# The second half's k, v and r kept in DRAM, and its recurrence set beside the first half's up projection

## The chip, the cores and the metric

The kernel runs on one core of a Trainium2 chip. The metric is the device time of one execution, in microseconds (us). TensorE (PE) multiplies, VectorE (DVE), ScalarE (ACT) and GpSimd (POOL) do the elementwise work, and SyncE (SP) issues every DMA. Each engine takes its own instructions strictly in the order in which they were laid down.

## What is computed

One layer of a block with a token mixer and a channel mixer over 1024 tokens of width 1024, all in float32:

```python
mod = silu(c) @ ada_w + ada_b                      # 6 vectors of 1024: modulation
sh_m, sc_m, gt_m, sh_f, sc_f, gt_f = split(mod, 6)
h = rms_norm(x, mix_pre_g) * (1 + sc_m) + sh_m
p = h @ w_in                                       # conv part, r, k, v, low-rank inputs
u = silu(layer_norm(causal_dwconv(u * sigmoid(u_gate), 31 taps)))
y = wkv7_scan(r, decay, k, v, kk, a)               # per head, state 64 x 64, token by token
y = (layer_norm(y) + bonus) * g
x = x + gt_m * rms_norm(concat([u, y]) @ w_out)
h = rms_norm(x, ffn_pre_g) * (1 + sc_f) + sh_f
z_gate, z_val = split(causal_dwconv(h @ w_up, 3 taps), 2)
x = x + gt_f * rms_norm((silu(z_gate) * z_val) @ w_down)
```

## The kernel before

The tokens are cut into two halves of 512 columns (`half` 0 and 1), and for the recurrence into four quarters of 256 (`q` 0 to 3), of four chunks of 64 tokens each. Everything lies with features on the 128 partitions and tokens along the free axis.

**Projections.** `project` (L147) multiplies one 128-row output tile. Float32 accuracy comes from two rounded parts of each operand (`hh`, `hl` for the activations, `wh`, `wl` for the weights) and three matmuls per 128 inputs, so a tile with 1024 inputs is 24 matmuls of 512 columns. `weight` (L135) loads 512 columns of weights (a chunk, two to a tile), ACT rounds them (L140), POOL takes the difference (L142); three buffers in a ring hold each of the three forms. The first half's `w_in` tiles are `lora`, `in_group` (k, v, r), `gate_in`, `glu`; then the same for the second half; then `out_proj`, `channel_in`, `up` (44 tiles `up_tile`) and `down`, for each half.

**Recurrence.** For each quarter `unit` does `prep` for two groups of heads (`w`, `a` and decay products, the kk norm, the chunk matrices `s`), `inverse` (a triangular inverse by DVE with a trip through DRAM, tensors `sa` and `sd`) and `merge` (`pt`, `hn`). Then `chain` walks the four chunks one after the other: `ch` (PE), `rs` (DVE L680 and ACT), `ch` again, `uv`, `y`, `zv`, each of which waits for the one ahead, and the state `zv` goes from quarter to quarter. `finish` normalizes y (`rx_y` at L173 is its first step) and writes it to DRAM (`mixed`, printed `mx`), where `mix_in` fetches it for `out_proj`.

**Convolution.** `conv` is a filler: DVE adds 93 taps of 3 channel tiles in a PSUM bank and ACT and POOL those of a fourth, some taps each time that `shifted`, `glu` or `up_tile` asks for a piece; `conv_norm` ends it.

**Modulation.** The first two of the six vectors come at the start (`ada_cols` on `ada1`). The other four are groups 0 to 3 of `ada2`: eight column blocks of eight 256 KB loads, each followed by one DVE step (`cacc_b` at L235 and L237), four small matmuls (`adrb`, L243) and an addition. They are the iterator `spare`, of which `project` takes `rate` steps after each weight chunk, and their loads share the weights' ring of three buffers (`wp`, tag `w`, printed `w_adb`).

**Order.** The program is written top to bottom (L888 to L966), but a scheduler lays down each engine's order, by a simulated time line and by priorities: earlier code goes first among what is ready, `first()` lifts a block by 1,000,000 places, `tc.high_priority(offset=500000)` by half as many. Before the change all of the recurrence, units and chains of all four quarters, is under `first()`. Buffers of a tag are taken in the order of the code. k and r tiles have three buffers each, v six, so the second half's k, v and r wait until the first half's quarters are done with theirs.

Of the kernel before, what the change touches and what calls it, by code (L numbers as in the profile page):

```python
# [10 lines left out]
ALU = mybir.AluOpType  # L11
# [56 lines left out]
def build(nc, tc, I, O):  # L68
# [151 lines left out]
    def ada_cols(j, src, name, pool, tag, bufs, apool, atag, b="m", share=()):  # L220
# [22 lines left out]
            TE.matmul(ps[:, m:m + 1], acc[:, m * P:(m + 1) * P], ones, start=True, stop=True)  # L243
        V.tensor_tensor(mod[:, j:j + 4], ps[:, 0:4], col("ada_b", j, 4), ALU.add)

    h = [None] * NK
    started = {}
    def start(z):
# [46 lines left out]
    def shifted(ps, half, j, out, n=P):  # L295

        q = tmp(f"s{half}_{j}", HT + 1)
        if half == 0:
            G.memset(q[:n, 0:1], 0.0)
        else:  # L300
            G.tensor_copy(q[:n, 0:1], carry_q[:n, j:j + 1])
        S.activation(q[:n, 1:], ps[:n], AF.Identity, scale=col("mu", j)[:n], bias=ZERO[:n])
        outs = out if isinstance(out, list) else [out]
        w = HT // len(outs)
        for i, o in enumerate(outs):
            V.scalar_tensor_tensor(o, ps[:n, i * w:(i + 1) * w], om[:n, j:j + 1], q[:n, i * w:(i + 1) * w], ALU.mult, ALU.add)
        if half == 0:
            G.tensor_copy(carry_q[:n, j:j + 1], q[:n, HT:HT + 1])
        next(filler[0], None)
# [80 lines left out]
            nc.sync.dma_start(mixed[half][ct], accs[ct])  # L390

    def lora(h, half):
        la = rw.tile([P, HT], F32, name=f"la{half}", tag="la", bufs=1)
# [59 lines left out]

    def v_tiles(half):

        new = lambda q, g: rw.tile([P, 2, QT], F32, name=f"v{2 * half + q}{g}", tag="v", bufs=6)
        order = ((0, 0), (0, 1), (1, 0), (1, 1)) if half == 0 else ((0, 0), (1, 0), (0, 1), (1, 1))
        t = {(q, g): new(q, g) for q, g in order}
        return [[t[q, g] for q in range(2)] for g in range(2)]

    def in_group(h, half, g, v):

        def new(x, q):
            if half == 0 and g == q == 1:
                return shared_slot({"k": "cacc1", "r": "cacc3"}[x], f"{x}{half}{g}")
            return rw.tile([P, 2, QT], F32, name=f"{x}{2 * half + q}{g}", tag=x, bufs=3)
        kvr = [[new("k", q) for q in range(2)], v, [new("r", q) for q in range(2)]]
        for i in range(2):
            p = 2 * g + i
            for x in range(3):  # L470
                shifted(in_tile(h, 10 + 3 * p + x, f"{'kvr'[x]}{half}{p}"), half, (4, 8, 0)[x] + p, [t[:, i] for t in kvr[x]])
        return kvr

    class Group:
# [287 lines left out]
    def x_rstd(half):  # L762

        acc = None
        for k in range(NK):
            x = tmp(f"xs{half}_{k}")
            nc.sync.dma_start(x, I["xT"][half, k])
            acc = square_sum(acc, x, k, f"x{half}")
        return rstd(acc, f"x{half}", ones, 1, 1.0 / D, EPS_RMS)

    def out_proj(half, ins):

# [105 lines left out]
    def unit(q, kvrs, la, before=None):  # L878

        pcs = wk.tile([P, 4, 4], F32, name=f"pc{q}", tag="pc", bufs=2)  # L880
        gs = [prep(q, g, kvrs[g], la, pcs, sas[q % 2]) for g in range(2)]
        inverse(q, sas[q % 2], sd[q % 2])
        if before:
            finish(q - 1, *before)
# [14 lines left out]
    with first():  # L899
        u0 = unit(0, kvrs, la)  # L900
        ys, zv = chain(0, *u0, None)
    ada = lambda gs: (x for g in gs for z in range(2)
                      for x in ada_cols(16 + 8 * g + 4 * z, I["ada2"][g, z], f"b{g}{z}", wp, "w", 3, cv, "cacc2"))
    spare, rate = ada(range(3)), 3
    for ct in range(4):
        glu(h, 0, ct)
        if ct == 0:
# [6 lines left out]
    for x in xs:  # L914
        V.tensor_tensor(x, x, rb, ALU.mult)
    h = [modulate(x, gm[:, k:k + 1], mod[:, k:k + 1], f"1_{k}") for k, x in enumerate(xs)]
    accs = [None] * 4
# [9 lines left out]
    with tc.high_priority(offset=500000):  # L927
        gates = gate_in(h, 1)
    for ct in range(4):
        glu(h, 1, ct)  # L930
        if ct == 0:
# [10 lines left out]
    for _ in spare:  # L942
        pass
# [6 lines left out]
    spare = ada((3,))  # L950
    filler[0] = conv(1, accs, 3)
    up(h, 0, lambda j: j == 18 and conv_norm(accs, 1, "s"))
    V.tensor_tensor(gpf, mod[:, 40:48], col("ffn_post_g", 0, 8), ALU.mult)
    oin = mix_in(1)
    cv.release()
# [68 lines left out]
```

## Time and profile before

| | us |
|---|---|
| median of 3 runs (1515.91 to 1520.45) | 1516.82 |
| the profiled execution | 1514.99 |
| its span, first to last instruction | 1513.2 |
| PE busy | 1377.6 |
| DVE busy | 958.3 |
| POOL busy | 796.4 |
| ACT busy | 645.9 |

An execution of 1514.99 us holds the span of 1513.2 and 1.8 us around it. A busy PE counts matmuls that overlap in its pipeline, so it says when PE had work, not that it was at its peak; the granted clock (PEclk) stands beside it, as a share of 2.4 GHz, and half of it is 1.2 GHz.

### The profile page before, as it was taken

The page shows a single profiled execution, that of the slowest core. Times are in us where ns is not written, and L with a number is a line of the kernel's source. Part 1 is how long each engine was busy: PE and PEld are TensorE (multiplying, and loading weights), DVE is VectorE, ACT ScalarE, POOL GpSimd, SP SyncE. Part 2 cuts the span into 40 slices and gives each one's busy share as a digit, 9 for nine tenths or more (in the row PEclk, how much of TensorE's full clock was granted, in tenths as well). Part 3 has the DMA queues.
Part 4 walks back from the last instruction along what each step waited for, and adds up shares of the span by engine and source line. Part 5 has one row for each costly group of instructions (what it writes and reads, how often), then busy time and mean ns, then how long its engine had stood idle before and what let it go on. Part 6 is the DMA issues. An engine that isn't in the chain of part 4 may idle for free.

```text
span 1513.2 us, 22723 instructions
## 1 busy us (share of the span) xinstructions
PE 1377.6 (91%) x8148; PEld 1111.8 (73%) x8148; DVE 958.3 (63%) x1449; ACT 645.9 (43%) x1126; POOL 796.4 (53%) x710
## 2 busy tenths in 40 slices
PE   3999868789889999769999999999998999999995
PEld 2777657677667777657788887788886888888884
DVE  8657857969989576587889965557117555552102
ACT  5344322355534454344455555654233444443221
POOL 2555413676755346435577764446545555554443
PEclk9998998899999999869999999999999999999997
DMA  9153645533224544834444335884335333333332
GB/s 358 58 167 101 176 140 160 175 81 105 63 60 118 162 138 107 219 116 128 138 132 133 118 120 179 303 274 134 101 97 185 98 97 97 97 95 93 94 95 73
DMA packets 161761, 203.78 MB, mean 135 GB/s; under 512 B 63536, under 2 KB 70320, under 8 KB 161648
## 3 DMA queue, kind: packets, MB, share of 16 engines
q1 hardware_dynamic: 161648, 202.33, 43.4%
q8 instruction: 64, 1.05, 0.3%
q14 instruction: 49, 0.40, 0.1%
HBM read 168.19 MB, written 34.08 MB: 134 GB/s over the span
## 4 chain that ended last, share of the span: by engine, by line
PE 66%; DVE 17%; DMA 10%; issue 3%; SPq 2%; POOL 2%; ACT 1%; DVEq 0%; POOLq 0%; ACTq 0%
PE up L158 10%; PE up L159 9%; PE up L160 9%; PE d L159 5%; PE d L160 5%; PE d L158 5%; DMA w_adb<-ada 3%; DVE cv L344 2%; PE o L159 2%; PE o L158 2%; PE o L160 2%; DMA aw_ada<-ada 2%; DVE cacc_b L237 1%; DVE rkp L528 1%; SPq L625 1%
## 5 line engine op out<-in xcount | busy, mean ns | idle before, releaser
L142 POOL TENSOR_TENSOR wl_up<-w_up,wh_up 128x512 fp32r<-128x512 f32 x176 | 240.3, 1370 | 157.5 <-ACT wh_up L140 150.7
L158 PE MATMUL up<-hh_f,wh_up 128*128 128x512 f32 x704 | 278.6, 396 | 10.2 <-DVE q_za L815 7.0
L159 PE MATMUL up<-hl_f,wh_up 128*128 128x512 f32 x704 | 277.0, 394 | 0.0
L160 PE MATMUL up<-hh_f,wl_up 128*128 128x512 f32 x704 | 276.6, 393 | 0.0
L140 ACT CAST wh_up<-w_up 128x512 fp32r<-128x512 f32 x176 | 108.7, 619 | 187.0 <-PE up L159 127.6
L142 POOL TENSOR_TENSOR wl_dn<-w_dn,wh_dn 128x512 fp32r<-128x512 f32 x96 | 116.9, 1220 | 118.0 <-ACT wh_dn L140 112.0
L158 PEld LDWEIGHTS up<-hh_f,wh_up 128*128 128x128 f32 x704 | 133.9, 190 | 40.6 <-issue 9.8
L160 PEld LDWEIGHTS up<-hh_f,wl_up 128*128 128x128 f32 x704 | 133.6, 190 | 28.2 <-issue 0.2
L159 PEld LDWEIGHTS up<-hl_f,wh_up 128*128 128x128 f32 x704 | 133.7, 190 | 27.6
L159 PE MATMUL d<-al,wh_dn 128*128 128x512 f32 x352 | 139.4, 396 | 0.0
L160 PE MATMUL d<-ah,wl_dn 128*128 128x512 f32 x352 | 139.4, 396 | 0.0
L158 PE MATMUL d<-ah,wh_dn 128*128 128x512 f32 x352 | 139.2, 395 | 0.0
L344 DVE SCALAR_TENSOR_TENSOR cv<-cu,pv,cv 128x512 f32<-128x512 f32 x174 | 130.4, 749 | 2.4
L140 ACT CAST wh_dn<-w_dn 128x512 fp32r<-128x512 f32 x96 | 56.1, 584 | 151.3 <-PE d L159 123.7
L860 DVE TENSOR_SCALAR mo_f<-d,mod 128x512 f32<-128x512 f32 x16 | 12.0, 749 | 170.4 <-ACT q_sqd L859 159.1
L810 DVE SCALAR_TENSOR_TENSOR q_za<-up,pv,q_za 128x510 f32<-128x510 f32 x88 | 65.6, 746 | 78.4 <-ACT q_za L808 78.4
L352 POOL TENSOR_TENSOR cacc<-cacc,ctmp 128x512 f32<-128x512 f32 x60 | 79.1, 1318 | 42.3 <-ACT ctmp L351 38.7
L159 PEld LDWEIGHTS d<-al,wh_dn 128*128 128x128 f32 x352 | 66.2, 188 | 16.0
L160 PEld LDWEIGHTS d<-ah,wl_dn 128*128 128x128 f32 x352 | 66.2, 188 | 15.8
L158 PEld LDWEIGHTS d<-ah,wh_dn 128*128 128x128 f32 x352 | 66.2, 188 | 15.8
L838 DVE SCALAR_TENSOR_TENSOR q_za<-q_th,q_za 128x512 f32<-128x512 f32 x44 | 57.7, 1312 | 30.3 <-ACT q_th L837 30.3
L815 DVE SCALAR_TENSOR_TENSOR q_za<-up,pv,q_za 128x511 f32<-128x511 f32 x88 | 65.9, 748 | 14.0 <-ACT carry_z L814 8.3
(383 smaller groups left out, 3024.5 us busy)
## 6 DMA issues: line engine op xcount, KB each, us to landing
w_up<-w_up SPq DMA_DIRECT2D x176, 256.0 KB, 2.8
w_dn<-w_down SPq DMA_DIRECT2D x80, 256.0 KB, 2.7
w_adb<-ada SPq DMA_DIRECT2D x64, 256.0 KB, 3.0
aw_ada<-ada SPq DMA_DIRECT2D x32, 256.0 KB, 5.4
w_o<-w_out SPq DMA_DIRECT2D x32, 256.0 KB, 3.5
act<-q_za SPq DMA_DIRECT2D x22, 256.0 KB, 2.0
ax<-act SPq DMA_DIRECT2D x22, 256.0 KB, 4.2
w_ug<-w_in SPq DMA_DIRECT2D x16, 256.0 KB, 3.1
```

The source lines that it names most:

```text
L140: S.copy(hi, w)
L142: e.tensor_tensor(lo, w, hi.bitcast(F32), ALU.subtract)
L158: TE.matmul(ps, wh[:, o], xh, start=k == 0, stop=False)
L159: TE.matmul(ps, wh[:, o], xl, start=False, stop=False)
L160: TE.matmul(ps, wl[:, o], xh, start=False, stop=k == K - 1)
L237: V.scalar_tensor_tensor(acc, w, sc[:, k:k + 1], acc, ALU.mult, ALU.add)
L344: yield V.scalar_tensor_tensor(o, u[:, k:k + HT], cw(ct, k), acc, ALU.mult, ALU.add)
L352: G.tensor_tensor(acc, acc, t, ALU.add)
L528: V.tensor_tensor(pic(rkp[x][:, :, 1 + hh, :])[r], part(kkn, x)[r], half(eprev, x)[r], ALU.mult)
L810: V.scalar_tensor_tensor(a[:, 2:], ps[:, 0:HT - 2], fw(0), a[:, 2:], ALU.mult, ALU.add)
L815: V.scalar_tensor_tensor(a[:, 1:], ps[:, 0:HT - 1], fw(1), a[:, 1:], ALU.mult, ALU.add)
L838: V.scalar_tensor_tensor(g_, t, 1.0, g_, ALU.add, ALU.mult)
```

## The change

It has five parts.

1. `ada_rest` takes the place of `ada_cols` for the four later vectors. Its loads go to five buffers of the convolution's pool that lie idle at the time (tags `ctmp` twice, `cu`, `cu3`, `cacc0`), four loads ahead of their use; the running sum lies in PSUM bank `v`. It is `spare` from the second group of the first half on (rate 1, then 2 in `glu`), not from `glu` on (rate 3). The small matmuls' result goes to PSUM bank `s`, of which there is one, where `prep` puts `w`, the kk norm and the bonus.
2. k, v and r of the second half are written to DRAM as whole tiles (`group_out`, 12 writes) and fetched by quarter (`group_back`, 12 loads); a second `la` buffer; v has five buffers.
3. `first()` is taken from units 2 and 3, chains 2 and 3 and the last `finish`; the `finish` inside a unit gets it. The half-as-high priority is taken from the second half's projections.
4. `out_proj(0)` and `channel_in(0)` stand ahead of chain 2, unit 3, chain 3 and the last `finish`, which in turn stand ahead of `up(h, 0)`.
5. The last vector's steps begin at the ninth pair of tiles of `up`, in the buffers of k. The row sums of `x_rstd` go to bank `y`.

```diff
+    def ada_rest(groups, slab, ahead, last, b):
+        todo = [(g, z, k) for g in groups for z in range(2) for k in range(NK)]
+        tiles = {}
...
+        for i in range(ahead):
+            fetch(i)
+        for i, (g, z, k) in enumerate(todo):
+            fetch(i + ahead)
+            w, name = tiles.pop(i), f"b{g}{z}"
+            if k == 0:
+                acc = bank(f"ad{name}", b)
+                V.tensor_scalar(acc, w, sc[:, 0:1], None, ALU.mult)
+            else:
+                o = last(name) if k == NK - 1 else acc
+                V.scalar_tensor_tensor(o, w, sc[:, k:k + 1], acc, ALU.mult, ALU.add)
+            if k == NK - 1:
+                j = 16 + 8 * g + 4 * z
+                ps = bank(f"adr{name}")
...
+    def group_out(h, g):
+        for i in range(2):
+            p = 2 * g + i
+            for x in range(3):
+                t = tmp(f"{'kvr'[x]}1{p}")
+                shifted(in_tile(h, 10 + 3 * p + x, f"{'kvr'[x]}1{p}"), 1, (4, 8, 0)[x] + p, t)
+                nc.sync.dma_start(kvd[g][x][:, :, i], t.rearrange("p (q t) -> p q t", q=2))
...
-    kvrs = [in_group(h, 0, g, vt[g]) for g in range(2)]
+    kvrs = [in_group(h, 0, 0, vt[0])]
+
+    ctags = ("ctmp", "cu", "ctmp", "cu3", "cacc0")
+    spare = ada_rest(range(3), lambda i, n: slot(cv, ctags[i % 5], n, 30 + HT if ctags[i % 5][:2] == "cu" else HT,
+                                                 2 if ctags[i % 5] == "ctmp" else 1)[:, :HT],
+                     4, lambda n: slot(cv, "cacc2", n), "v")
+    kvrs.append(in_group(h, 0, 1, vt[1]))
...
-    with tc.high_priority(offset=500000):
-        la = lora(h, 1)
-    vt = v_tiles(1)
-    with tc.high_priority(offset=500000):
-        kvrs = [in_group(h, 1, g, vt[g]) for g in range(2)]
-    with first():
-        u2 = unit(2, kvrs, la, (u1[0], ys))
...
+    la = lora(h, 1)
+    for g in range(2):
+        group_out(h, g)
+
+    u2 = unit(2, [group_back(2, g) for g in range(2)], la, (u1[0], ys))
...
-    with first():
-        ys, zv = chain(2, *u2, zv)
-        u3 = unit(3, kvrs, la, (u2[0], ys))
-        ys, zv = chain(3, *u3, zv)
-        finish(3, u3[0], ys)
...
     with first():
         h = channel_in(0, acc, "m")
+    ys, zv = chain(2, *u2, zv)
+    u3 = unit(3, [group_back(3, g) for g in range(2)], la, (u2[0], ys))
+    ys, zv = chain(3, *u3, zv)
+    finish(3, u3[0], ys)
     accs = [None] * 4
...
```

What the scheduler makes of it is seen at two places. The first is DVE's queue where `prep` of the first quarter begins. `einv_cs00` is that unit's running sum of decays, `k00`, `v00` and `r10` are tiles of the projections. Before:

```order
L306 SCALAR_TENSOR_TENSOR r10_588<-p_first12_303,om_93,q_s0_0_655 128x256
L498 SCALAR_TENSOR_TENSOR einv_cs00_1172<-cst_78,einv_cs00_1172 128x64 x8
L306 SCALAR_TENSOR_TENSOR k00_585<-p_first13_322,om_93,q_s0_5_679 128x256
L306 SCALAR_TENSOR_TENSOR k10_586<-p_first13_322,om_93,q_s0_5_679 128x256
L506 COPY pc0_1169<-ep00_1190 128x8
L306 SCALAR_TENSOR_TENSOR v00_581<-p_first14_341,om_93,q_s0_9_703 128x256
```

In the changed kernel, the same sum (now L547), among steps of the modulation (`adb11`) and of the second half's square sum (`q_accx1`):

```order
L265 TENSOR_SCALAR adb11_2129<-cacc0_adb11_0_2025,sc_97 128x512
L808 TENSOR_TENSOR q_accx1_1085<-q_accx1_1085,q_sqx11_1089 128x512
L268 SCALAR_TENSOR_TENSOR adb11_2129<-ctmp_adb11_1_2028,sc_97,adb11_2129 128x512
L268 SCALAR_TENSOR_TENSOR adb11_2129<-cu_adb11_2_2049,sc_97,adb11_2129 128x512
L268 SCALAR_TENSOR_TENSOR adb11_2129<-ctmp_adb11_3_2052,sc_97,adb11_2129 128x512
L547 SCALAR_TENSOR_TENSOR einv_cs00_1250<-cst_78,einv_cs00_1250 128x64 x4
L268 SCALAR_TENSOR_TENSOR adb11_2129<-cu3_adb11_4_2127,sc_97,adb11_2129 128x512
L547 SCALAR_TENSOR_TENSOR einv_cs00_1250<-cst_78,einv_cs00_1250 128x64 x4
L337 SCALAR_TENSOR_TENSOR k01_758<-p_k03_918,om_93,q_s0_7_968 128x256
```

The sum moved from behind the fourth tile of the projections to behind the tenth, and 28 steps of the modulation now stand ahead of its first part. The second place is PE's queue at the first step of the last chain (`ch3_0`, second product). Before, just ahead of the first `up` tile, beside the norm of `channel_in` (`c_f0`, `rb_f0`):

```order
L169 MATMUL c_f0_6618<-cst_78,q_accf0_6566 128x1 x4
L684 MATMUL ch3_0_5839<-rs3_0_5841,at30_5397 64x64 x4
L684 MATMUL ch3_0_5839<-rs3_0_5841,at31_5523 64x64 x4
L187 MATMUL rb_f0_6627<-cst_78,r_f0_6623 128x128 x4
L692 MATMUL y3_0_5840<-uv3_0_5822,bkt030_5375 64x64 x4
L692 MATMUL y3_0_5840<-uv3_0_5822,bkt031_5501 64x64 x4
L158 MATMUL up00_6680<-hh_f0_0_6640,wh_up00_0_6683 128x512
```

In the changed kernel it stands between the eleventh and the twelfth `up` tile (`up05`, `up027`):

```order
L159 MATMUL up05_7228<-hl_f0_7_5620,wh_up05_4_7249 128x512
L160 MATMUL up05_7228<-hh_f0_7_5617,wl_up05_4_7251 128x512
L733 MATMUL ch3_0_6423<-rs3_0_6425,at30_5981 64x64 x4
L733 MATMUL ch3_0_6423<-rs3_0_6425,at31_6107 64x64 x4
L158 MATMUL up027_7284<-hh_f0_0_5582,wh_up027_0_7287 128x512
L159 MATMUL up027_7284<-hl_f0_0_5585,wh_up027_0_7287 128x512
```

The chain moved behind eleven tiles of the up projection, and all of unit 3's products with it.

## Rows read from the trace of the kernel before

**Rows 1.** The page: span, engines' busy time, granted clock in 40 slices.

```profile
span 1513.2 us, 22723 instructions
PE 1377.6 (91%) x8148; PEld 1111.8 (73%) x8148; DVE 958.3 (63%) x1449; ACT 645.9 (43%) x1126; POOL 796.4 (53%) x710
...
PEclk9998998899999999869999999999999999999997
```

**Rows 2.** Windows: stretch, length, busy PE PEld DVE ACT POOL, clock, DMA share, GB/s.

```profile
0.00:77.00 77.00, 50.04 (x197) 40.65 (x198) 55.99 (x99) 34.05 (x52) 31.80 (x46) 0.98 0.58 205
77.00:222.90 145.90, 122.80 (x806) 95.19 (x807) 99.14 (x183) 54.09 (x96) 62.40 (x64) 0.92 0.52 152
222.90:492.10 269.20, 240.21 (x1879) 190.17 (x1879) 230.03 (x381) 118.13 (x210) 161.33 (x147) 0.91 0.37 107
492.10:620.60 128.50, 124.45 (x1112) 97.43 (x1111) 80.04 (x155) 58.06 (x111) 62.51 (x50) 0.99 0.48 136
620.60:687.10 66.50, 45.89 (x543) 39.05 (x542) 45.97 (x69) 23.84 (x43) 26.21 (x21) 0.72 0.55 166
687.10:733.30 46.20, 43.80 (x336) 35.28 (x335) 40.41 (x56) 24.29 (x48) 24.28 (x19) 0.96 0.47 145
733.30:947.50 214.20, 209.16 (x921) 171.79 (x919) 170.87 (x217) 113.20 (x208) 142.65 (x104) 0.98 0.43 137
947.50:1513.20 565.70, 541.29 (x2365) 442.26 (x2364) 235.81 (x294) 220.26 (x361) 285.20 (x261) 0.98 0.41 128
```

**Rows 3.** Timeline of PE at the borders of stages: start us, us, instruction.

```profile
70.64 1.13 PE L492 MATMUL w<-la,w2a 64*128 64x256 f32 x4
...
620.28 0.40 PE L160 MATMUL o<-hh_o,wl_o 128*128 128x512 f32 x1
...
943.62 0.39 PE L158 MATMUL o<-hh_o,wh_o 128*128 128x512 f32 x1
...
992.56 0.39 PE L160 MATMUL o<-hh_o,wl_o 128*128 128x512 f32 x1
992.79 0.40 PE L158 MATMUL d<-ah,wh_dn 128*128 128x512 f32 x1
```

**Rows 4.** Timeline of DVE: chain steps, norms of y, drains of up tiles.

```profile
222.88 0.42 DVE L680 COPY rs<-ch 64x256 f32<-64x256 f32 x1 [0.86 <-PE ch L679]
...
492.07 0.17 DVE L173 TENSOR_SCALAR rx_y<-c_y 128x16 f32<-128x16 f32 x1 [2.29 <-PE c_y L169]
...
530.93 0.42 DVE L680 COPY rs<-ch 64x256 f32<-64x256 f32 x1 [2.55 <-PE ch L679]
...
657.70 0.41 DVE L680 COPY rs<-ch 64x256 f32<-64x256 f32 x1
...
687.12 0.75 DVE L810 SCALAR_TENSOR_TENSOR q_za<-up,pv,q_za 128x510 f32<-128x510 f32 x1
...
733.34 0.17 DVE L173 TENSOR_SCALAR rx_y<-c_y 128x16 f32<-128x16 f32 x1
...
947.53 0.74 DVE L810 SCALAR_TENSOR_TENSOR q_za<-up,pv,q_za 128x510 f32<-128x510 f32 x1
```

**Rows 5.** By tile `w_adb`: the modulation's DVE step, min/median/max ns.

```profile
L237 DVE SCALAR_TENSOR_TENSOR cacc_b<-w_adb,sc,cacc_b x56: 720/752/1873, 145.0 to 728.9; 128x512 f32<-128x512 f32 x56
```

**Rows 6.** Waits of DVE, 77 to 222.9 us: total, times, longest.

```profile
DVE cacc_b L237 <- DMA w_adb<-ada: 9.3, 8, 1.9
DVE kkn L515 <- PE rb_kk L187: 8.4, 3, 5.0
DVE r L306 <- ACT q_s L302: 5.5, 1, 5.5
```

**Rows 7.** The page: DMA issues with size and median us to landing.

```profile
w_adb<-ada SPq DMA_DIRECT2D x64, 256.0 KB, 3.0
aw_ada<-ada SPq DMA_DIRECT2D x32, 256.0 KB, 5.4
```

**Rows 8.** Timeline of SP: the last writes of the first half's mixed tiles.

```profile
521.31 1.52 SPq L390 DMA_DIRECT2D mx<-cacc  x2
```

More of the change, by code (lines that the diff above doesn't have):

```diff
@@ L244, in ada_cols, with fetch @@
         V.tensor_tensor(mod[:, j:j + 4], ps[:, 0:4], col("ada_b", j, 4), ALU.add)
+    def ada_rest(groups, slab, ahead, last, b):
+        todo = [(g, z, k) for g in groups for z in range(2) for k in range(NK)]
+        tiles = {}
+        def fetch(i):
+            if i < len(todo):
+                g, z, k = todo[i]
+                tiles[i] = slab(i, f"adb{g}{z}_{k}")
+                nc.sync.dma_start(tiles[i], I["ada2"][g, z, k])
+        for i in range(ahead):
[12 more added lines that the diff above has]
+                ps = bank(f"adr{name}")
+                for m in range(4):
+                    TE.matmul(ps[:, m:m + 1], o[:, m * P:(m + 1) * P], ones, start=True, stop=True)
+                V.tensor_tensor(mod[:, j:j + 4], ps[:, 0:4], col("ada_b", j, 4), ALU.add)
+            yield
     h = [None] * NK
@@ L392, in lora @@
     def lora(h, half):
-        la = rw.tile([P, HT], F32, name=f"la{half}", tag="la", bufs=1)
+        la = rw.tile([P, HT], F32, name=f"la{half}", tag="la", bufs=2)
         shifted(in_tile(h, 8, f"la{half}"), half, 12, la)
@@ L454, in v_tiles @@
     def v_tiles(half):
-        new = lambda q, g: rw.tile([P, 2, QT], F32, name=f"v{2 * half + q}{g}", tag="v", bufs=6)
-        order = ((0, 0), (0, 1), (1, 0), (1, 1)) if half == 0 else ((0, 0), (1, 0), (0, 1), (1, 1))
-        t = {(q, g): new(q, g) for q, g in order}
+        new = lambda q, g: rw.tile([P, 2, QT], F32, name=f"v{2 * half + q}{g}", tag="v", bufs=5)
+        t = {(q, g): new(q, g) for q, g in ((0, 0), (0, 1), (1, 0), (1, 1))}
         return [[t[q, g] for q in range(2)] for g in range(2)]
@@ L471, in in_group, with group_back @@
                 shifted(in_tile(h, 10 + 3 * p + x, f"{'kvr'[x]}{half}{p}"), half, (4, 8, 0)[x] + p, [t[:, i] for t in kvr[x]])
+        return kvr
+    kvd = [[dr.tile([P, 2, 2, QT], F32, name=f"{x}d{g}") for x in "kvr"] for g in range(2)]
+    def group_out(h, g):
[5 more added lines that the diff above has]
+                nc.sync.dma_start(kvd[g][x][:, :, i], t.rearrange("p (q t) -> p q t", q=2))
+    def group_back(q, g):
+        kvr = []
+        for x in range(3):
+            t = rw.tile([P, 2, QT], F32, name=f"{'kvr'[x]}{q}{g}", tag="kvr"[x], bufs=(3, 5, 3)[x])
+            nc.sync.dma_start(t, kvd[g][x][:, q % 2])
+            kvr.append({q % 2: t})
         return kvr
@@ L768, in x_rstd @@
             acc = square_sum(acc, x, k, f"x{half}")
-        return rstd(acc, f"x{half}", ones, 1, 1.0 / D, EPS_RMS)
+        return rstd(acc, f"x{half}", ones, 1, 1.0 / D, EPS_RMS, b="y")
     def out_proj(half, ins):
@@ L883, in unit @@
         if before:
-            finish(q - 1, *before)
+            with first():
+                finish(q - 1, *before)
         merge(gs, sd[q % 2])
@@ L901, in build @@
         ys, zv = chain(0, *u0, None)
-    ada = lambda gs: (x for g in gs for z in range(2)
-                      for x in ada_cols(16 + 8 * g + 4 * z, I["ada2"][g, z], f"b{g}{z}", wp, "w", 3, cv, "cacc2"))
-    spare, rate = ada(range(3)), 3
+    rate = 2
     for ct in range(4):
@@ L916, in build @@
     h = [modulate(x, gm[:, k:k + 1], mod[:, k:k + 1], f"1_{k}") for k, x in enumerate(xs)]
+    for _ in spare:
+        pass
     accs = [None] * 4
@@ L919, in build @@
     filler[0] = conv(0, accs, 8)
[L920 to L928 removed]
+    la = lora(h, 1)
+    for g in range(2):
+        group_out(h, g)
+    u2 = unit(2, [group_back(2, g) for g in range(2)], la, (u1[0], ys))
+    gates = gate_in(h, 1)
     for ct in range(4):
@@ L948, in build, with between @@
         h = channel_in(0, acc, "m")
+    ys, zv = chain(2, *u2, zv)
+    u3 = unit(3, [group_back(3, g) for g in range(2)], la, (u2[0], ys))
+    ys, zv = chain(3, *u3, zv)
+    finish(3, u3[0], ys)
     accs = [None] * 4
-    spare = ada((3,))
     filler[0] = conv(1, accs, 3)
-    up(h, 0, lambda j: j == 18 and conv_norm(accs, 1, "s"))
+    def between(j):
+        nonlocal spare
+        if j == 8:
+            spare = ada_rest((3,), lambda i, n: slot(rw, "k", n, bufs=3), 2, lambda n: slot(cv, "cacc2", n), "c")
+        if j == 18:
+            conv_norm(accs, 1, "s")
+    up(h, 0, between)
     V.tensor_tensor(gpf, mod[:, 40:48], col("ffn_post_g", 0, 8), ALU.mult)
```

2 lines of the change are left out of this document (removed).

## The prediction

> **What bounds the kernel now.** I read the page first: PE is busy for 1377.6 of 1513.2 us, so what a change can give is PE's idle time and its time at the half clock, and the slices of the granted clock say that nearly all of the latter lies in the first half of the span [rows 1]. Then the windows, cut at the milestones that the change moves [rows 2]. The reader is to see three kinds of stretch. From 947.5 us on (`out_proj(1)`, `down`, `up(1)`, `down`) PE is busy for 541.3 of 565.7 us; no line of it is touched. Between the first chain step (222.9) and the norm of the second quarter (492.1) DVE is busy for 230.0 of 269.2 us, 85%: there the chain, the conv taps and the modulation queue on DVE, and PE, busy by the page, stands at a clock of 0.91. And from 620.6 to 687.1, between `out_proj(0)` and the first drained `up` tile, PE is busy for 45.9 of 66.5 us at a clock of 0.72: `channel_in` and the merge of the last unit are both chains of short waits, and no large product lies beside them.
>
> The time is a path of five legs to the drain of the last `up` tile of the first half, at 947.5 us [rows 3, 4]; behind it 565.7 us stay as they are. The legs now: (a) to the first chain step, 222.9; (b) on to the norm of quarter 1, 269.2; (c) on to the last product of `out_proj(0)`, 128.5; (d) on to the first drained `up` tile, 66.5; (e) on to the last one, 260.4 [rows 2 to 4].
>
> **Leg a, the modulation's loads taken forward.** By the first chain step the new order has DVE do 48 steps of the modulation where it did 24 (24 more), and also the 16 operations on the second half's x, 11 conv taps and 3 more `glu` products that used to come later. At 0.75 us a step [rows 5], and as much for the others, which are of the same 512 columns, that is 54 x 0.75 = 40 us; 28 scans and other small operations at 0.3 us, an estimate, bring it to some 48. DVE had 145.9 - 99.1 = 46.8 us of idle time between 77 and 222.9 [rows 2], part of it waits for these very loads (9.3 us), which four loads ahead and own buffers should end, part of it (8.4 and 5.5) waits for PE and ACT within the unit [rows 6]. All of the idle time used: 222.9 + 48 - 46.8 = 224 us. None: 271. Against the low end speaks that unit 0 now starts late: its `w` takes PSUM bank `s`, which the first two modulation results hold until their 16 loads are summed; in PE's order it comes some six and a half tiles later than now, 24 matmuls of 0.23 us each [rows 3], about 36 us after the 70.6 of now. I take 250, half of the idle time.
>
> In the same leg DMA carries about 110 transfers of 256 KB in some 125 us, 230 GB/s, as much as the first 77 us do (205 GB/s) [rows 2]. There a load lands after 5.4 us, later 3.0 [rows 7]. A weight chunk feeds PE for 2.7 us and the ring holds three, 8.2 us, against 5.4 plus a rounding and a difference of about 1.9: covered, by under a microsecond. The Trainium skill (DMA: Bandwidth & Descriptors, "Latency and other measured facts") puts an HBM access at 0.2 us on average and 2 us under high load. An estimate by that page adds another 1.8 us to the 5.4, a shortfall of about 1 us in three chunks, 14 us of PE over 42 chunks; it would not reach the chain, which is the path here, and the sum by it is the same.
>
> **Leg b, the same chain with less beside it.** What went ahead of the first chain step is gone from here: 24 steps, 16 x operations, 11 taps and some small ones, 53 of DVE's operations in all; at the 48 us of leg a that leaves some 180 of its 230. The second half's k, v and r no longer wait for the first half's buffers, so PE has `w_in` tiles to do throughout. If DVE keeps its 85%, 180/0.85 = 211 us. The floor is the pace of the two later quarters, which had little beside them: from the first step of chain 2 (530.9) to that of chain 3 (657.7) 126.8 us, and from there to the norm 75.6 [rows 4], together 202. The ceiling is the 269 of now. I take 218, near the rows with the same load on DVE.
>
> The 12 writes and 12 loads of k, v and r cost SP about 0.33 us each to issue and 6 MB; the loads have the rest of chain 1 to land, and a tile drained by one operation of 512 columns replaces two of 256. I cost this at nothing. If a load waits for its buffer at the head of SP's queue, the weights behind it wait too: up to a few us, in the range of this leg.
>
> **Leg c, nothing left between finish and out_proj.** Now 3 1/2 pairs of `glu` tiles lie between the norm of quarter 1 and `out_proj(0)`. In the new order all of them come before. What is left is latency: the last mixed tile was written 521.3 + 1.5 - 492.1 = 30.7 us behind the norm [rows 4, 8], landing, reload and split take some 6 us, then eight tiles, which took 943.6 to 992.8 = 49.2 us in the second half with the same start [rows 3]. Less 2 us for products on the conv half that can go first: 84 us, between 78 and 92. PE idles for most of the first 35 us, a new wait that the sum holds.
>
> **Leg d, channel_in beside another chain.** Chain 2 and `prep` of unit 3 now run where merge 3 ran. Between the norm of `out_proj(0)` and the first drain DVE has 110 instructions in its queue against 65 now (the difference: `prep`'s products `rkp`, `bk`, `mq` and the chain's); 45 more at the 0.60 us of leg b's mix, 230.0 us for 381, are 27 us. 20.5 us of this stretch are idle on DVE [rows 2], so the leg lies between 66.5, if short ones fill the gaps, and 93.5, if none is filled; `channel_in` has the higher priority now, which speaks against the upper end. I take 80. The Trainium skill (TensorE: Matmul & The Clock Gate, Part 1) calls the cost of the clock's ramp less than 1% of a typical span; the slices of the clock [rows 1] and the stretch at 0.72 [rows 2] show more here: 0.72 over 66.5 us is 37 us at the lower of the two levels, 1.2 GHz, up to 19 us of time in this leg alone. By the page a change in this could move the sum by at most 15 us; I add no term for it, by either.
>
> **Leg e, the recurrence beside `up`.** Unit 3's rest, chain 3 and the last finish add DVE work to a stage that PE fills at 24 x 0.23 us a tile. From the first drain to the norm of quarter 3 the new order holds 192 DVE instructions, at 0.60 (leg b) to 0.72 us (687 to 733, 40.4 for 56) 115 to 138 us, say 130; at the 40.4/46.2 = 87% that DVE reached in 687 to 733 [rows 2] that is 150 us, while PE has 479 large matmuls (109 us) and 376 small ones, 129 together at some 0.05 us. From there on DVE has 138 at 0.79 us (170.9 for 217), 109 us, and PE 534 large ones and few small, 124 with the conv norm's short wait 127. Together 277, between 261 (PE alone, 253, plus 8) and 290 (DVE at 80% in the first stretch). The chain itself has some 120 us of slack: it ends at the 22nd of 44 tiles.
>
> **Sum.** 250 + 218 + 84 + 80 + 277 = 909 us, 38.5 less than 947.5. The profiled execution, 1514.99 = 1513.2 + 1.8, becomes 1476.5; it lies 1.8 us below the median of the runs, so the median to expect is **1478 us**.
>
> **Rivals.** *The recurrence does not speed up* (the slower side). Unit 0 starts 36 us late behind the 16 loads, all of which arrives at the first chain step, and the two quarters of leg b still take 135 us each because their steps wait for PE's and ACT's answers, not for DVE's queue. Then a is 259, b 269, and the sum 528 + 84 + 80 + 277 = 969, 21.5 later: 1538. For it: 14% of DVE's time in leg b is idle, and three engines answer one another at each step. Against it: the last quarter went through its four steps in 75.6 us [rows 4]. It decides at a + b = 506.5, that is 14 us behind the 492.1 of now. *DVE gives it back.* Legs d and e near their upper ends and a + b at 480: 480 + 84 + 93 + 290 = 947, no change, 1517. For it: DVE is at 85% and more wherever the chain has company. *The early work packs.* The idle time in leg a is absorbed and the chain goes at its floor: 228 + 204 + 82 + 72 + 265 = 851, 96 less: 1420. For it: four fifths of DVE's idle time in leg a are waits of one or two us that more ready work can fill. *The change does not do what it says*, the chain still the last to end: it would have to slip by 100 us beside `up`; under 2 in 100, within the slower case.
>
> **How the numbers follow.** Forecast with its spread (1440 to 1512) 0.63; packed early work (below 1440) 0.10; given back (1512 to 1521) 0.10; slower recurrence (above 1521) 0.17. About 0.3% is what a measurement of this kernel can tell from no change, 1512.3 to 1521.4. So faster 0.73, same 0.10, slower 0.17. The terms' own bounds, a 224 to 271, b 202 to 269, c 78 to 92, d 66.5 to 93.5, e 261 to 290, not all at one end, give about 35 us to either side; to leave out no more than 2 in 10 the range goes up to the given-back case and a little beyond: 1438 to 1524.
>
> **What would show it.** In the profile after: the first chain step (`rs`) at 240 to 260 us, later than now; the norm of quarter 1 at 455 to 485, earlier than now, with DVE's busy share of 77 to 250 above 80%; no `glu` tile behind that norm and PE idle ahead of `out_proj(0)` for 25 us or more; its last product near 552; the first drained `up` tile near 632 and the last near 909; the last `finish` done long before. Wrong is the first step if `rs` comes after 265, the second if the norm of quarter 1 lies behind 500, the last if `up` takes over 295 us.

## The result and the profile after

The changed kernel takes 1494.72 us (median of 4 runs, 1493.66 to 1497.85), the kernel before, run beside it, 1518.63: a ratio of 0.9846 with a 95% interval of 0.9819 to 0.9872, 24 us faster. The forecast was faster, 1478, with a range of 1438 to 1524. The profiled execution of after took 1497.85, its span is 1496.0; it is the longest of the four, 3.1 us above their median. So the two profiled spans lie 17 us apart, and the legs below add up to that.

The windows of after, cut at the same milestones as [rows 2] (stretch, length, busy time of PE, PEld, DVE, ACT, POOL with their instructions, granted clock, DMA share, GB/s):

```profile
0.00:77.00 77.00, 48.90 (x190) 40.36 (x191) 58.58 (x97) 32.02 (x48) 31.56 (x43) 0.96 0.66 232
77.00:249.30 172.30, 165.89 (x1051) 132.23 (x1050) 134.50 (x248) 74.88 (x130) 94.69 (x93) 0.94 0.63 194
249.30:477.70 228.40, 206.13 (x1745) 160.71 (x1744) 184.58 (x312) 106.37 (x192) 141.91 (x131) 0.96 0.40 113
477.70:554.70 77.00, 66.58 (x428) 51.24 (x428) 26.01 (x48) 32.47 (x54) 24.73 (x20) 0.89 0.54 164
554.70:636.90 82.20, 63.92 (x576) 50.90 (x577) 66.94 (x113) 33.37 (x66) 40.67 (x33) 0.73 0.29 98
636.90:794.00 157.10, 151.71 (x1224) 120.66 (x1223) 131.96 (x192) 78.97 (x153) 91.77 (x70) 0.99 0.41 120
794.00:929.80 135.80, 129.40 (x581) 106.02 (x579) 104.79 (x139) 69.58 (x128) 82.82 (x60) 0.99 0.48 155
929.80:1496.00 566.20, 540.99 (x2364) 441.63 (x2364) 236.75 (x294) 220.85 (x362) 286.01 (x261) 0.98 0.40 128
```

The milestones on DVE's timeline, which answer to [rows 4]:

```profile
249.25 0.41 DVE L729 COPY rs<-ch 64x256 f32<-64x256 f32 x1
...
477.72 0.17 DVE L173 TENSOR_SCALAR rx_y<-c_y 128x16 f32<-128x16 f32 x1 [1.54 <-PE c_y L169]
...
929.83 0.73 DVE L859 SCALAR_TENSOR_TENSOR q_za<-up,pv,q_za 128x510 f32<-128x510 f32 x1
```

| leg (us) | before | predicted | after |
|---|---|---|---|
| a, to the first chain step | 222.9 | 250 | 249.3 |
| b, to the norm of quarter 1 | 269.2 | 218 | 228.4 |
| c, to the last product of `out_proj(0)` | 128.5 | 84 | 77.0 |
| d, to the first drained `up` tile | 66.5 | 80 | 82.2 |
| e, to the last drained `up` tile | 260.4 | 277 | 292.9 |
| sum | 947.5 | 909 | 929.8 |

Behind the last drain 566.2 us remain, 565.7 before. Every leg moved the way that was forecast; of the 38.5 us of the sum 17.7 came. The legs, though, are not where the time is made. The reader is to see that PE is busy for 97 and 95% of the two stretches of leg e, and for 96 and 90% from 77 us to the end of legs a and b. So a second account was made, from the starts of all of PE's records: the large products (512 columns) at the 0.227 us by which one follows the other, the records of the small ones at 0.03, as in the block of them that is shown below, and what remains: waits, the half clock, small products that take longer, and slow changes from one kind to the other.

| leg (us) | before: large, small, remaining | after: large, small, remaining |
|---|---|---|
| a | 107, 16, 87 | 147, 18, 71 |
| b | 132, 39, 98 | 114, 37, 77 |
| c | 67, 25, 37 | 44, 7, 26 |
| d | 11, 15, 41 | 11, 16, 56 |
| e | 230, 7, 23 | 231, 23, 38 |
| sum | 547, 101, 287 | 547, 101, 269 |

(13 us ahead of the first product come to both.) The products are the same in both kernels: 2408 large ones and 3376 records of small ones stand in either trace up to the last drain. What the change is worth is the last column, 18 us less remaining: legs a, b and c lose 48, legs d and e get 30 back. A leg that became shorter because its products went elsewhere has won nothing.

### The profile page after: what moved, and what is told of

Same layout as the page of the kernel before. It is cut to its first block, busy times and chain, and to the rows that moved or that the text cites. A ratio compares the mean times of both kernels' runs of the same rounds, so it can differ in the third digit from the quotient of the medians.

```text
span 1496.0 us, 22755 instructions
## 1 busy us (share of the span) xinstructions
PE 1373.5 (92%) x8148; PEld 1103.8 (74%) x8148; DVE 944.1 (63%) x1437; ACT 648.5 (43%) x1126; POOL 794.2 (53%) x710
## 4 chain that ended last, share of the span: by engine, by line
PE 68%; DVE 19%; DMA 7%; issue 3%; ACT 1%; SPq 1%; POOL 0%; DVEq 0%; POOLq 0%; ACTq 0%
PE up L158 9%; PE up L159 9%; PE up L160 9%; PE d L160 5%; PE d L159 5%; PE d L158 5%; DVE cv L375 4%; PE o L160 2%; PE o L159 2%; PE o L158 2%; PE s L599 1%; DMA aw_ada<-ada 1%; DVE rkp L577 1%; DVE t_dx L656 1%; DVE bk L579 1%
## 5 line engine op out<-in xcount | busy, mean ns | idle before, releaser
L158 PE MATMUL up<-hh_f,wh_up 128*128 128x512 f32 x704 | 279.3, 397 | 10.4 <-DVE q_za L864 10.4
L158 PEld LDWEIGHTS up<-hh_f,wh_up 128*128 128x128 f32 x704 | 133.8, 190 | 39.8 <-issue 6.7
L158 PE MATMUL d<-ah,wh_dn 128*128 128x512 f32 x352 | 139.2, 395 | 0.0
L158 PEld LDWEIGHTS d<-ah,wh_dn 128*128 128x128 f32 x352 | 66.1, 188 | 15.9
```

The source lines that it names most:

```text
L158: TE.matmul(ps, wh[:, o], xh, start=k == 0, stop=False)
```

## Leg e: is it DVE's queue?

The prediction made the first stretch of leg e DVE-bound. In `conv`:

```diff
                 for k in range(1, KC):
+                    if half and 0 < k % 3 and k < KC - 1:
+                        yield None
+                        continue
```

> The changed kernel, but 60 of the 93 taps that VectorE adds for the second half's convolution (each third one stays) are left out of the computation; they lie in leg e, 45 us of VectorE's time at 0.75 us each. Theory (leg e is set by TensorE: 1019 large products of 0.227 us, 231 us, and the recurrence's small ones, of which more lie here than before, with short waits): leg e falls from 293 by 3 to 12 us only, time 1483 to 1492. Rival (the prediction's step: VectorE's queue sets the first stretch of leg e): the first stretch falls from 157 to about 125 to 135, leg e to 260 to 270, time 1463 to 1475.

Measured: 1493.03 us, ratio 0.9874 (0.9838 to 0.9909), no better than the changed kernel, though its convolution leaves out 60 taps. Its windows of leg e, divided at the norm of quarter 3 as above:

```profile
635.20:784.70 149.50, 146.05 (x1206) 117.71 (x1203) 107.76 (x163) 76.18 (x147) 87.47 (x67) 0.98 0.44 128
784.70:923.30 138.60, 134.11 (x603) 109.94 (x602) 77.42 (x110) 72.17 (x132) 88.91 (x63) 0.99 0.46 149
```

DVE is busy for 185 us instead of 237, and the leg is 288.1 instead of 292.9. So PE sets it, busy for 98 and 97% of the two stretches. The term of the prediction that failed is its size of PE's work in the first stretch: 376 small products at 0.05 us. On PE's timeline of after (start, us, instruction) one block of the chain's small products stands among `up` products like this:

```profile
703.84 0.39 PE L158 MATMUL up<-hh_f,wh_up 128*128 128x512 f32 x1
704.07 0.39 PE L159 MATMUL up<-hl_f,wh_up 128*128 128x512 f32 x1
704.38 0.27 PE L698 MATMUL vb<-cst,v 64*64 64x64 f32 x1
704.39 0.27 PE L699 MATMUL vb<-cst,v 64*64 64x64 f32 x1
704.49 0.22 PE L698 MATMUL vb<-cst,v 64*64 64x64 f32 x1
704.50 0.22 PE L699 MATMUL vb<-cst,v 64*64 64x64 f32 x1
...
704.84 0.22 PE L698 MATMUL vb<-cst,v 64*64 64x64 f32 x1
704.85 0.22 PE L699 MATMUL vb<-cst,v 64*64 64x64 f32 x1
705.00 0.50 PE L160 MATMUL up<-hh_f,wl_up 128*128 128x512 f32 x1
```

`values` issues 8 products for a chunk, and the trace has 16 records: a small product leaves two. Inside the block a pair follows the other after 0.06 us (0.10 the first time), near the 0.05 of the forecast; but at both borders time is lost: 0.31 us from the last large product to the first small one instead of 0.23, and 0.15 back. The block takes 705.00 - 704.07 = 0.93 us, less the large product's own 0.23: 0.70, 0.09 for each of the 8. For the whole stretch (636.9 to 794; 1224 records, 488 of them large) 488 large products at 0.227 are 111 us and 368 small ones at that price 33, together 144, which leaves 13 for waits; the forecast had 129 for PE. Summed over all 30 blocks of the stretch, the time from the last large product to the next one, less 0.23, is 39 us with the waits inside the blocks: 0.11 a product. DVE's own number was right, 132 us busy against 130.

## Which part brings the gain

The parts were taken apart one at a time. First the early loads alone, in the kernel before:

```diff
...
-    kvrs = [in_group(h, 0, g, vt[g]) for g in range(2)]
+    kvrs = [in_group(h, 0, 0, vt[0])]
...
+                     4, lambda n: slot(cv, "cacc2", n), "v")
+    kvrs.append(in_group(h, 0, 1, vt[1]))
...
-    spare, rate = ada(range(3)), 3
+    rate = 2
...
```

> Part 1 of the change alone, in the kernel before: the later modulation weights in own buffers, four loads ahead, from the second group on; order, priorities and buffers of k, v and r as before. Theory (two gains that add up): the steps leave leg b (first chain step to norm of quarter 1) for leg a, so a goes to 240 to 250, b to 225 to 245, a + b to about 478 as in the changed kernel, and the rest stays as before: last drained up tile near 933, time 1503 (1495 to 1510). Rival (all of the gain is in the new order and the parked k, v, r): the late start of unit 0 costs leg a its 26 us and leg b gives nothing back, because it waits for answers of PE and ACT: a + b 500 to 520, time 1517 to 1540.

Measured: 1537.77, ratio 1.0151 (1.0116 to 1.0187), slower. Legs a to e are 258.5, 243.2, 127.2, 76.1, 264.6, the last drain is at 969.6. The rival had the time, but for another reason than it said: b did give 26 back, and a took 36. Among PE's waits in leg a stood a line that this edit should not have touched:

```profile
PE c_x L169 <- DVE q_accx L790: 5.6, 1, 5.6
```

`c_x` is the row sums of the second half's x, and in this run they still go to bank `m`, of which the tiles have two. The changed kernel sends them to `y`, an edit to which the prediction gave no term. So this edit was added to the run:

```diff
-        return rstd(acc, f"x{half}", ones, 1, 1.0 / D, EPS_RMS)
+        return rstd(acc, f"x{half}", ones, 1, 1.0 / D, EPS_RMS, b="y")
```

> The run with part 1 alone, and with it the one other small edit that the changed kernel has: the row sums of the second half's x go to PSUM bank y, not to bank m, which the projections' tiles use. Theory (in that run TensorE waited 5.6 us at the row sums for VectorE's squares, with a tile's bank held since they were laid down; with 24 more steps in VectorE's queue this wait grows): leg a falls from 258 to 240 to 250, a + b to 480 to 490, time 1510 to 1525, 12 to 25 us below that run. Rival (part 1 alone is slower because of the chain's priority over the tiles and of the steps in VectorE's queue): within 5 us of that run, 18 us or more above the kernel before.

Measured: 1518.86, ratio 1.0018 (0.9998 to 1.0038), 19 us below the run without it; the wait is gone. Its windows:

```profile
0.00:231.80 231.80, 193.37 (x1142) 157.25 (x1142) 166.62 (x306) 98.03 (x161) 114.96 (x132) 0.96 0.65 213
231.80:474.20 242.40, 205.88 (x1710) 160.97 (x1711) 195.39 (x356) 107.48 (x193) 135.16 (x125) 0.89 0.26 67
474.20:635.80 161.60, 147.72 (x1440) 118.15 (x1439) 90.60 (x172) 65.51 (x125) 62.60 (x51) 0.95 0.47 138
```

The norm of quarter 1 comes at 474.2, earlier than in the changed kernel, and nothing is won: leg c is 161.6. Without parking, the second half's tiles are left for later: PE is busy for 205.88 of 242.40 us in b, at a clock of 0.89, and has their products in c. Why the one bank costs 19 us here, more than the wait itself, was not taken further; whether it matters within the full change was not tried.

Next the change without its early loads:

```diff
-                     4, lambda n: slot(cv, "cacc2", n), "v")
...
-    rate = 2
+    spare, rate = ada(range(3)), 3
...
-        if j == 8:
-            spare = ada_rest((3,), lambda i, n: slot(rw, "k", n, bufs=3), 2, lambda n: slot(cv, "cacc2", n), "c")
+        if j == 0:
+            spare = ada((3,))
...
```

The last vector goes back to the weights' ring too, from the first pair of `up` tiles on.

> The changed kernel without its part 1: the later modulation weights come through the weights' ring again, from the glu tiles on, three steps a chunk, the rest of them before out_proj(0); the last vector from the first up tile on. Theory (two gains that add up): a as before, 220 to 228; b 255 to 270, as DVE keeps its 24 steps there; c 75 to 85, d 78 to 85, e 285 to 300; last drained up tile near 937, time 1505 (1496 to 1514). Rival (the early loads make the rest possible: without them DVE and the ring hold up the tiles that now run beside the chain): c keeps glu tiles or waits for the modulation, a + b + c above 590, time 1517 or more.

Measured: 1536.75, ratio 1.0172 (1.0118 to 1.0226). Legs 221.4, 287.4, 78.4, 82.1, 295.5. The rival is right in the time, not in its place: leg c is 78.4, with no `glu` tile to speak of left in it, and 31 of the 35 us that the last drain comes later than in the changed kernel are in a + b, 508.8 against 477.7. What the loads do there is seen in ACT's waits (us in total, times, longest). In the kernel before, legs a and then b:

```profile
ACT wh_u L140 <- DMA w_u<-w_in: 14.8, 4, 6.0
ACT wh_ug L140 <- DMA w_ug<-w_in: 7.4, 2, 5.5
...
ACT wh_u L140 <- DMA w_u<-w_in: 18.1, 4, 5.4
...
ACT wh_ug L140 <- DMA w_ug<-w_in: 10.2, 3, 6.0
```

These are 50 us in which ACT stands at the head of its queue for the weights of `glu` tiles, and the chain's copies stand behind that in the same queue. They are the tiles among which `ada_cols` takes three loads a chunk from the weights' ring. In the changed kernel the same two lines, in both legs together, come to 2.7 us:

```profile
ACT wh_u L140 <- DMA w_u<-w_in: 2.1, 1, 2.1
...
ACT wh_u L140 <- DMA w_u<-w_in: 0.6, 1, 0.6
```

Without the early loads they are back, 26 and 30.5 us. So the ring alone was tried, in the kernel before: own buffers (`own` hands out the five idle ones), the steps' place in the program unchanged.

```diff
...
-            w = slot(pool, tag, f"ad{name}_{k}", bufs=bufs)
+            w = bufs(f"ad{name}_{k}") if callable(bufs) else slot(pool, tag, f"ad{name}_{k}", bufs=bufs)
...
-    spare, rate = ada(range(3)), 3
+    spare, rate = ada(range(3), own), 3
```

> The kernel before, with one thing changed: the loads of the three early modulation vectors go to the five idle buffers of the convolution's pool instead of the weights' ring; the steps stay where they stand in the program (from the glu tiles on, three a chunk), their sum and results stay in their old places; 38 steps instead of 24 now stand ahead of the first chain step. Theory (it is the ring that the change frees: in the kernel before ACT waits 22 us in leg a and 28 us in leg b for the weights of the glu tiles to land, in the changed one for none of them): these waits fall below 15 us together, a + b from 492 to 470 to 484, time 8 to 20 us below the kernel before. Rival (the ring costs nothing, since other tiles fill in; the slower run with early loads alone was slower because steps on VectorE's queue ahead of unit 0 delay the chain): a grows by 8 to 15 us, b falls by less, time between 4 us below and 20 us above the kernel before.

Measured: 1509.28, ratio 0.9951 (0.9928 to 0.9973). The waits for `w_u` and `w_ug` fall from 50 us to 5.3, a + b to 479.9, as the theory has it; the time is 7.4 us lower, just short of the 8 to 20 that were expected. Leg c is 135.9 against 128.5, though it has only 3 large products more (296 against 293); where its other 7 us come from was not settled.

The parking undone, all else as changed:

```diff
...
-    for g in range(2):
-        group_out(h, g)
-    u2 = unit(2, [group_back(2, g) for g in range(2)], la, (u1[0], ys))
+    vt = v_tiles(1)
+    kvrs = [in_group(h, 1, g, vt[g]) for g in range(2)]
+    u2 = unit(2, kvrs, la, (u1[0], ys))
...
```

> The changed kernel with k, v and r of the second half kept on chip as before (three buffers of k and r, six of v, one of la), all else as changed. Theory (the parking is what lets the second half's tiles run beside chains 0 and 1): the tiles wait for buffers until quarter 1 is through with them, so glu tiles slip behind the norm of quarter 1, leg c grows from 77 to 100 to 130, time 1515 to 1550. Rival (the order alone brings the gain, the transfers through DRAM are an extra): legs within 8 us of the changed kernel's 249, 229, 77, 82, 293, time 1488 to 1500.

Measured: 1505.25, ratio 0.9941 (0.9921 to 0.9962), between the two cases. Legs 241.1, 238.0, 84.8, 81.3, 290.9. The theory had the place and not the size: c grows by 8, not by 25 to 50. By the ratios (0.9941 against 0.9846) parking is worth some 14 us of the 24; the profiled spans, 1503.8 and 1496.0, show 8.

And the order undone, with early loads and parking:

```diff
...
+    with first():
+        ys, zv = chain(2, *u2, zv)
+        u3 = unit(3, [group_back(3, g) for g in range(2)], la, (u2[0], ys))
+        ys, zv = chain(3, *u3, zv)
+        finish(3, u3[0], ys)
     gains()
     with tc.high_priority(offset=500000):
         acc = out_proj(0, mix_in(0))
...
```

> The changed kernel with its early loads and k, v, r in DRAM, but with units 2 and 3, chains 2 and 3 and the last finish at the highest priority and ahead of out_proj(0) again, and the second half's projections at the middle one, as before the change. Theory (putting the recurrence beside the up projection moves its time from leg c to legs d and e and gains little by itself: 51 less in c, 16 more in d, 32 more in e): a + b 475 to 495, c 115 to 135, d 66 to 80, e 260 to 268, time 1490 to 1510. Rival (the parked tiles all run early, so the later chains then have nothing beside them, and the order is what makes the change worth anything): c above 150 or a + b above 500, time 1520 or more.

Measured: 1497.88, ratio 0.9899 (0.9878 to 0.9920). Legs 233.4, 251.5, 121.5, 64.2, 258.0, last drain at 928.7, 1.1 us ahead of the changed kernel's. This is the theory, with d and e 2 us shorter still. The part of the change that is the largest to read, the recurrence beside `up`, takes 7 us off a + b and 44 off leg c and gives 18 and 35 back in d and e. By the ratios it is worth some 8 us (0.9899 against 0.9846, the intervals only just apart), but the profiled spans, 1494.9 here and 1496.0 in the changed kernel, show nothing of it. Whether this part gains anything is not shown.

Together, as ratios to the kernel before: early loads alone 1.015 (with the one bank 1.002), order and parking without them 1.017, loads and order 0.994, loads and parking 0.990, all 0.985. The order alone and the parking alone were not run. The worth of a part depends on the others: the early loads take 3.2% off what order and parking make, and nothing off the kernel before.

## Legs a and b: the bank, and a buffer

In the changed kernel `w` of unit 0 starts at 105.7 (70.6 before), behind the modulation's result in the one bank `s`.

```diff
-                ps = bank(f"adr{name}")
+                ps = bank(f"adr{name}", "m")
```

> The changed kernel, but the small matmuls' result of the modulation goes to PSUM bank m (two buffers, in turn with the projections' tiles) instead of the one bank s. Theory (unit 0 starts late because its w waits for bank s until 16 loads are summed): w of unit 0 starts at 70 to 90 instead of 105.7, leg a falls from 249 by 10 to 25 us; half of that is given back in leg b, where the DVE work then lies: time 1480 to 1490. Rival (leg a is set by DVE's queue, in which the steps lie ahead of the unit's, whatever the bank): leg a moves by under 5 us, time 1491 to 1498; or, since bank m now waits for 8 steps in the middle of the tiles, up to 10 us longer.

Measured: 1502.31, ratio 0.9922 (0.9897 to 0.9947), slower than the changed kernel. Leg a is 225.0, as the theory has it, b 247.4, and e 300.8, 8 longer. Bank `m` only for the vectors that come early:

```diff
-                ps = bank(f"adr{name}")
+                ps = bank(f"adr{name}", "s" if g == 3 else "m")
```

> As the run with the result of the modulation's small matmuls in bank m, but only for the three vectors that come early; the last vector, in leg e, keeps bank s. Theory (in that run legs a and b together became 5 us shorter, and leg e 8 us longer because there the tiles' bank waited for steps of the last vector): a near 225, a + b 470 to 474, e back to 290 to 295, time 1485 to 1491. Rival (leg e's growth there came with the other order of all that follows, not from the bank): e stays near 300 and the time at 1496 to 1503.

Measured: 1491.88, ratio 0.9853 (0.9832 to 0.9874). Legs 225.3, 247.8, 76.7, 84.1, 290.6: e is back, so it was the bank in leg e. The first product on `w` of unit 0 in the changed kernel, and in this run:

```profile
105.67 1.13 PE L541 MATMUL w<-la,w2a 64*128 64x256 f32 x4
...
72.04 1.13 PE L541 MATMUL w<-la,w2a 64*128 64x256 f32 x4
```

In both, 48 steps of the modulation stand ahead of the first chain step, 24 more than before. So it is the bank, not the added steps, that makes leg a longer: it accounts for 24 of the 26 us. But leg a, 24 us shorter here, gives 19 of it to leg b, the last drain comes 5 us earlier (924.6), and the ratio shows no gain: PE does tiles while unit 0 waits. Then the buffer that `finish` waits for:

```diff
-        sq = [slot(rw, "t", f"ysq{s.n}", bufs=2) for s in gs]
+        sq = [slot(rw, x, f"ysq{s.n}") for x, s in zip(("kkn", "a"), gs)]
```

> The changed kernel, but the squares with which finish begins go to the buffers of kkn and a, not to the two of tag t, which the inverse of the next unit uses just then (ACT waited 3.8 and 1.1 us for it ahead of the norm of quarter 1, and TensorE 9 us for ACT). Theory (this wait is on the path of leg b): norm of quarter 1 4 to 8 us earlier, 470 to 474, the rest as it was, time 1486 to 1491. Rival (the engines' orders put the norm behind other work that ends no earlier; or kkn's buffer, now read later, holds up the next prep): norm within 2 us of 477.7 or later, time 1493 to 1500.

Measured: 1492.58, ratio 0.9867 (0.9847 to 0.9886); the norm of quarter 1 at 475.8, 1.9 us earlier: the rival.

## Leg d, and the three edits together

```diff
...
     def between(j):
...
+        if j == 1:
+            u3 = unit(3, [group_back(3, g) for g in range(2)], la, (u2[0], ys))
+            ys, zv = chain(3, *u3, zv)
+            finish(3, u3[0], ys)
...
```

> The changed kernel with unit 3, chain 3 and the last finish written behind the first pair of up tiles instead of ahead of it, so that the first tiles come before unit 3 in every queue. Theory (leg d is 82 us, against 66.5 before the change, because TensorE's queue has products of unit 3 ahead of the first up tile, one of which waits 7.7 us for VectorE): d falls to 68 to 74, e grows by 3 to 6 us, as its small products now lie there, time 4 to 10 us below the changed kernel. Rival (leg d is the chain of channel_in itself, and unit 3 was in its gaps): d within 4 us of 82, e up by as much as its small products need, time the same or up to 8 us longer.

Measured: 1489.08, ratio 0.9813 (0.9775 to 0.9852), not to be told from the changed kernel's 0.9846. Leg d is 80.6, as the rival has it (leg e, 288.6, did not grow as either case expected), for the product that waits stands where it stood, since the scheduler fills the gaps of `channel_in` with it from either place. The line is the same in both kernels' PE waits of leg d:

```profile
PE bo L587 <- DVE r L585: 7.7, 1, 7.7
```

Last, the bank for the early vectors, the buffers for `finish` and unit 3's later place in one run:

> Three edits of single runs together, on the changed kernel: the early modulation results in bank m, the squares of finish in buffers of their own, unit 3 and what follows it behind the first pair of up tiles. Theory (their gains at the last drained up tile, 5.2, 3.5 and 8.0 us of 929.8, lie in different legs, a + b, b and e, and so add up): last drained up tile at 911 to 917, time 1478 to 1486, ratio to the kernel before about 0.977. Rival (each only moves TensorE's idle time to another place, so that no more than the largest of them is left): last drained up tile at 920 to 926, ratio 0.981 to 0.986.

Measured: 1490.98, ratio 0.9847 (0.9820 to 0.9873), the last drain at 920.5: the rival. Legs 225.2, 228.3, 94.7, 72.7, 299.6. The windows of the first three legs for the products of L158 alone, which are a third of the large ones of the projections (stretch, length, PE and PEld busy with their instructions, clock, DMA share, GB/s):

```profile
0.00:225.20 225.20, 70.48 (x169) 33.87 (x169) 0.95 0.64 204
225.20:453.50 228.30, 72.42 (x175) 33.55 (x175) 0.96 0.42 124
453.50:548.20 94.70, 36.54 (x88) 17.54 (x88) 0.86 0.56 162
```

The same of the changed kernel:

```profile
0.00:249.30 249.30, 85.30 (x209) 40.75 (x209) 0.95 0.64 206
249.30:477.70 228.40, 64.02 (x160) 29.66 (x159) 0.96 0.40 113
477.70:554.70 77.00, 25.43 (x64) 12.09 (x64) 0.89 0.54 164
```

The norm of quarter 1 comes 24 us earlier, with 344 of these products done instead of 369. 25 x 3 at 0.227 us are 17 us, and leg c is 17.7 longer. A milestone that comes earlier only because PE has done less by then is no gain. None of these versions is measurably faster than the changed kernel.

## Why the prediction came out as it did

**Leg a**, right at 249.3, but by luck, for its sum is not what happened. The 48 steps stand ahead of the chain step and unit 0 starts late, as forecast. But DVE's added work is 38 us, not 48 (193.1 busy against 155.1; the 28 other small operations are not there, 60 or so instructions came in all where 82 were counted), and of its 46.8 us of idle time only 9 are used (172.30 - 134.50 leaves 37.8), not half. The two misses cancel. What sets the leg is the wait for bank `s`, which the text named only as a reason against the low end: without it the leg is 225.3, with the same 48 steps. DVE's busy share from 77 us on is 78%, just under the 80 that were named.

**Leg b**, 10.5 too short. 184.6 us of DVE work were there, 180 expected; the share was 81%, not 85. That a + b fell at all (477.7 against 492.1) rests in the main on a cause that the sum didn't have, the weights' ring: with the loads out of it and the steps in their old place a + b is 479.9. The text called the weights covered "by under a microsecond", with a ring of three, and did not count that in the kernel before, among the `glu` tiles, three of four loads in that ring are the modulation's; ACT's waits show it, and they were not read. The prediction's estimate by the Trainium skill (DMA: Bandwidth & Descriptors, "Latency and other measured facts") had loads under high load cost some 14 us more in leg a; ACT's waits for weights there, from 77 us on, are 9.6 us in all (6.1, 2.1 and 1.4), against 26 before, so no such loss shows, and the own buffers outweigh it if there is one.

**Leg c**, right in kind (77 against 84): no `glu` tile is left in it. But PE is not idle for 25 us there, as the signs had it; it is busy for 66.6 of the 77. Its first two products of `out_proj(0)` come at 492.7 and 493.0, the third at 502.95, and from there on they follow one another. The window up to there:

```profile
477.70:503.00 25.30, 16.24 (x195) 13.63 (x195) 12.51 (x24) 10.84 (x17) 3.25 (x3) 0.70 0.77 216
```

So the latency is 25 us, not 35, and PE is busy for 16 of it, at a clock of 0.70, most of it with products of unit 2's merge. That the leg became 51 us shorter is in part no gain: by the norm of quarter 1 the changed kernel has done 369 L158 products, the one before 336 (150 and 186); 33 x 3 at 0.227 are 22 us. In the runs with the old order or without parking c is 85 to 162.

**Leg d**, right (82.2 against 80), though the run that was meant to shorten it shows that the other chain stands in its gaps. The lower bound was loose: 27 us of work less 20.5 of idle time leave 73, not 66.5. The clock there is 0.73, [rows 2] have 0.72. The Trainium skill (TensorE: Matmul & The Clock Gate, Part 1) puts the ramp under 1% of a typical span, and speaks there of the warm-up; the mean clock of the whole span is 0.954 here, by which some 9% of it lie at the lower level, so the figure does not cover what this kernel loses behind its start. The clock of this stretch stayed as it was, and no term for it was needed.

**Leg e**, 16 too short, is the largest miss, and the leg is PE's, not DVE's: taking a fifth of DVE's work away shortened it by 5 us of 293. Of the miss 7 us lie in the first stretch (157 against DVE's 150), where the term "376 small ones at some 0.05" of PE's work failed: measured, they cost 0.09 each in an undisturbed block and 0.11 with the waits. The other 9 lie in the second (136 against 127): 531 large products take 120.5 us, as forecast, and 48 small records with PE's waits take 15 where 6 were put.

**The rivals.** The time lies in the forecast's own spread, above its middle, between it and "DVE gives it back": a + b is 477.7 and e 292.9, near that case's 480 and 290, c and d are 7 and 11 below it; but in leg e it is PE that took the time back. "The recurrence does not speed up" was decided at 506.5 as put: a + b without the early loads is 508.8, and that run is slower than before.

## What to carry to other kernels

When one engine is busy for nine tenths of the time, keep its account (the work that both versions share, and the time that remains) beside the path of milestones: an earlier milestone counts only with the work done by then. Price small products by a whole block on the timeline, from the last large product to the next one, and read who waits for a ring of buffers before loads are moved out of it. Check a leg that came out right by its terms as well: here two misses cancelled. The worth of a part depends on the others, and the edit that looked least, one PSUM bank, cost 19 us in one combination.

## What the runs showed of the hardware

Going from large products to small float32 ones of 64 columns and back costs PE time: 0.31 us to the first small one, where large ones follow one another at 0.23, and 0.15 us from the last small one to the next large one. Inside a block they follow one another after 0.06, so a block loses some 0.2 us at its borders. 30 blocks lie in the first stretch of leg e, nearly all with borders like these: some 6 us of PE, an estimate.
